# Around the end of attention: weight splits ahead of the adaLN chunks, low parts on VectorE, and 0.47 side steps per attention step for the last chunks

## The chip, the cores and the metric

One core of a Trainium2 chip runs the whole program. The metric is device time in microseconds of one execution; three runs of the kernel before gave 868.11 at the median (866.49 to 872.79).

## The reference, cut to what matters

The reference is one step of a two-layer trunk over 640 tokens (512 latent tokens, 128 context tokens) of width 1024. Layer 0 is gated attention with 16 query heads over 4 key/value heads, layer 1 a gated linear recurrence. Each layer is modulated by shift, scale and gate that come from a conditioning vector (adaLN):

```python
mod = jax.nn.silu(cond) @ w + b                 # w: 1024 x 3072, per layer
sh, sc, g = jnp.split(mod, 3, axis=-1)
h = x * (1.0 + sc) + sh
q, k, v, gate = split(h @ w_in)                  # q: 1024 wide, k and v: 256, gate: 1024
o = softmax(q @ k.T / 8) @ v                     # latent rows read 128 context + 512 latent keys
out = (o * silu(gate)) @ w_out                   # w_out: 1024 x 1024
x = layer_norm(1.414 * x + g * out) * gain + bias
```

Layer 1 does the same with a recurrence in the place of the softmax. The outputs are the tokens after both layers, the context's keys and values, and the final states of the recurrence.

## The kernel before

All matrix products with weights are made of three passes: a number is held as a high part, rounded to a short form, and a low part, which is the rest, and TensorE adds high by high, high by low and low by high. So every weight piece and every activation has to be **split**: ScalarE (ACT) casts the high part, and another engine subtracts it from the number to get the low part. `split_piece` (L219) does this for a weight piece of 128 x 1024: it takes the next raw piece out of a queue, casts it (L225), and subtracts on the engine that it is given (L226). `split_act` (L947) does the same for activations (cast L948, subtraction L949). `split_gs` (L951) splits the gated attention output `gs`, 8 slices of 128 x 640, into `hhi` and `hlo`, and gives the subtraction to GpSimd (POOL). `wo_gen` (L939) splits the 8 pieces of the output projection `attn_w_out` (two halves `nh` of the columns, four pieces each, into the tiles `wohi` and `wolo`) and lets POOL and VectorE (DVE) take turns.

**Raw pieces** come by DMA from the SP queue in one fixed order, the list `order` (L368 to L385); `pump` issues the next load whenever fewer than five loaded pieces are waiting, into a ring of six buffers. Who takes a piece must take them in that order.

**Attention** (`att_gen`, L850) goes through four groups of heads, c = 0 to 3, which the text calls quarters; a quarter has one unit for the context tokens and eight for the latent tokens. A unit has fronts (scores `sc` on TensorE (PE) at L732 and L733, row maxima `nm` on DVE at L826, exponentials `p` on ACT at L829, reciprocals `rc` on DVE at L833, and the scaling of `p` on POOL at L834) and backs (transposes `pt` on PE at L841, which ACT or DVE copies to `pts` at L737, then products with the values, `pot` at L759, and the multiplication with the gate on DVE at L764, which finishes a part of `gs`). Fronts run two units ahead of backs.

**Side work** is woven into attention's steps: `weave(att, side, SIDE_B)` (L984) makes 0.85 steps of side work for each step of attention. The side work is a list of items in order: for c = 1, 2 and 3 the projection of the next quarter's queries (`q_gen`, products `qmm`, statistics `sq`, `ss`, `rs_t`, `rstd`, then rotation, split `qs`, transposes `qps` on PE at L589 and their copy to `X` at L591), mixed with some adaLN chunks; then item "a", the last seven adaLN chunks (`ada_gen`: products `adaps` at L266, their copy to `row` at L280, two small products at L289, results `shsc` and `gcol`), which may not start before quarter 3's backs do; then item "w" (`prefetch_gen`), which splits the first two pieces of `attn_w_out`; then item "s", the first six slices of `split_gs`.

Everything up to the block's end (L993) lies in one block whose instructions a scheduler reorders with a timeline of its own, so what the code weaves is a wish, and the order on each engine is the scheduler's. Each engine then works through its own list strictly in order.

After the block's end come the last two slices of `split_gs`, the six other pieces of `attn_w_out`, and the output projection of layer 0 (`outp`, L1005 to L1009): 24 products of 128 x 512 for each token tile `tt` and half `nh`, in the order (0,0), (1,0), (0,1), (1,1), (2,0) and so on. `Norm.part` (L1026) reads a finished half out of PSUM on DVE: `y` at L1030 multiplies it by the gate, L1031 adds the residual `x`, L1033 takes statistics. Both halves of a token tile lie in one PSUM tile. The first two pieces of `rec_w_in` (tiles `rhi` and `rlo`, the weights of layer 1) are split in the same place.

Of the kernel before, what the change touches and what calls it, by code (L numbers as in the profile page):

```python
# [40 lines left out]
D_SCALE = 2  # L41
D_OUTS = 2
SIDE_T = 1.0
SIDE_B = 0.85
MIX = 0.36
D_GLA = 6.0
D_LEV = 2.3
# [38 lines left out]
def weave(main, side, ratio):  # L86
    acc = 0.0
    for _ in main:
        acc += ratio
        while acc >= 1.0:  # L90
            acc -= 1.0
            side.step()
# [40 lines left out]
def hybrid_step(ctx: ExitStack, tc: tile.TileContext, a: dict, o: dict):  # L133
    nc = tc.nc
# [85 lines left out]
    def split_piece(hi, lo, src, lo_eng=None, pinned=False):  # L220
        pump()
        got, raw = ahead.popleft()
        assert got == src, (got, src)
        pin = tc.keep_in_program_order if pinned else lambda ins: ins
        pin(nc.scalar.copy(hi, raw))  # L225
        pin((lo_eng or nc.gpsimd).tensor_tensor(lo, raw, hi.bitcast(F32), ALU.subtract))  # L226
        pump()
# [139 lines left out]
    def ada_pieces(part):  # L367
        return [p for l, c in part for p in pieces(f"ada_w{l}", c)]  # L368
# [4 lines left out]
    for c in range(3):  # L373
        order.extend(pieces("attn_w_in", c + 1))
        order.extend(ada_pieces(ADA_B[c]))
    order.extend(ada_pieces(ADA_B[3]))
    order.extend(("attn_w_out", nh, i) for nh, i in PIECES)
    order.extend(("rec_w_in", h, i) for h in range(RH) for i in range(5))
    order.extend(("rec_w_out", nh, i) for nh, i in OUT1)
    for n, back in ((0, 2), (1, 1)):  # L380
# [196 lines left out]
    def q_split(r, tt0, n, odd, X, alloc):  # L577
        s2 = prep.tile([P, 1024], F32R, tag="s2", name="qs2", bufs=2)
        rv = view(r, 0, [[HD, 4 * n], [1, HD]])
        hv = view(s2, HD * odd, [[P, 4 * n], [1, HD]])  # L580
        nc.scalar.copy(hv, rv)
        nc.vector.tensor_tensor(view(s2, HD * (1 - odd), [[P, 4 * n], [1, HD]]), rv, hv.bitcast(F32), ALU.subtract)

        def back(i):
            pt = alloc("qps")
            pr = pt[:].bitcast(F32R)
            for h in range(4):
                s = i * 512 + h * P
                nc.tensor.transpose(pr[:, h * P:(h + 1) * P], s2[:, s:s + P], identr)  # L589
            c0 = (tt0 + i) * P  # L590
            nc.scalar.copy(X[:, :, c0:c0 + P], pt[:].rearrange("p (a b) -> p a b", a=4))  # L591
        return back
# [7 lines left out]
    def q_gen(c, X):  # L600
        w = Weights("attn_w_in", c, (nc.vector, nc.vector))
        yield
        yield
        pend = None
        for tt0, n in UNITS:
            ps = yield from tok_unit(w, tt0, n, "qmm")
            rstd = rms_stat(ps, n)
            yield
            if pend:
                for i in range(pend[1]):  # L610
                    pend[0](i)
                    yield
            else:
                yield
            yield
            qn = rms_apply(ps, n, rstd)
            r = rope_apply(qn, tt0, n, cosq, sinq, qg)
            yield
            pend = (q_split(r, tt0, n, c % 2, X, bank1), n)
        yield  # L620
        for i in range(pend[1]):
            pend[0](i)
            yield
# [315 lines left out]
    def wo_gen(layer, pieces, wpool):  # L939
        for nh, i in pieces:  # L940
            hi = wpool.tile([P, 1024], F32R, tag=f"wohi{nh}{i}", name="wohi")
            lo = wpool.tile([P, 1024], F32R, tag=f"wolo{nh}{i}", name="wolo")
            wo[nh, i] = tuple(t[:].rearrange("p (k n) -> p k n", k=2) for t in (hi, lo))
            split_piece(hi, lo, ("attn_w_out" if layer == 0 else "rec_w_out", nh, i), (nc.gpsimd, nc.vector)[i % 2])
            yield

    def split_act(dst_hi, dst_lo, src, eng=None):  # L947
        nc.scalar.copy(dst_hi, src)  # L948
        (eng or nc.vector).tensor_tensor(dst_lo, src, dst_hi.bitcast(F32), ALU.subtract)  # L949

    def split_gs(ks):  # L951
        for k in ks:
            split_act(hhi[:, k, :], hlo[:, k, :], gs[:, k, :], nc.gpsimd)
            yield

    ws = ExitStack()
# [23 lines left out]

    for c in range(1, 4):
        side.items.append((f"q{c}", mixed(q_next(c), ada_gen(ADA_B[c - 1])), lambda c=c: front_of[0] >= c - 1))
    side.items.append(("a", ada_gen(ADA_B[3]), lambda: back_of[0] == 3))
    side.items += [("w", prefetch_gen()), ("s", split_gs(range(6)), lambda: back_of[0] == 3)]  # L984
    weave(att, side, SIDE_B)
    side.finish()
    ph.close()
    right.close()
# [226 lines left out]
    for tt, nh in ((0, 0), (1, 0), (0, 1), (1, 1), (2, 0), (2, 1), (3, 0), (3, 1), (4, 0), (4, 1)):  # L1215
        if nh == 0:
            norms[tt] = Norm(0, tt)
        out_mms(norms[tt].ps[nh], tt, nh, hhi, hlo)
        norms[tt].part(nh, norms[tt].ps[nh])
        if nh == 1:  # L1220
            with tc.high_priority() if tt == TS else nullcontext():
                norms[tt].finish()
            if tt > 1:
                h1_tile(tt - 1, norms[tt - 1].y)
            elif tt == 1:
                h1_tile(0, norms[0].y)
# [375 lines left out]
```

## Time and profile before

| what | us |
|---|---|
| median of three runs | 868.11 |
| the profiled execution | 868.67 |
| its span in the profile | 866.9 |
| PE busy | 827.0 (95%) |
| DVE busy | 528.8 (61%) |
| ACT busy | 382.5 (44%) |
| POOL busy | 205.9 (24%) |
| last quarter of attention, from the first of its adaLN chunks to the output projection | 311.4 to 356.3 |

Between 500 and 800 us the share of PE's busy time is 100% in each stretch of 100 us, so what is gained or lost before comes out at the end, as long as PE has its work there. The stretch that the change touches lies between 240 and 390 us. There PE's busy share falls below 90% only in a few slices of 10 us; a table of such slices gives, for each engine, the busy time and in brackets the number of instructions, and then the TensorE clock that was granted, as a share of the full one. A list of waits tells for whom an engine stood still, in us: the total, how often, and the longest. A timeline row has the start, the busy time, the engine, the line, the operation with output and input tiles, and in square brackets the idle time just before and who ended it.

### The profile page before, as it was taken

The numbers are of one execution on the slowest core, as the hardware profiler recorded it, in microseconds if no ns is written. First come the engines' busy times: TensorE is split into PE (matmuls) and PEld (weight loads), VectorE is DVE, ScalarE is ACT, GpSimd is POOL, SyncE is SP. The second block draws the span as 40 slices with busy tenths as digits, with TensorE's granted clock in tenths as the row PEclk, the third lists the DMA queues.
The fourth block names the chain that finished last, engine by engine and source line by source line (L and its number), as shares of the span: only waits on it lengthen the run. The fifth ranks groups of instructions, "written<-read, shape, count | busy, mean of one in ns | idle before, by whom it ended". The sixth has DMA issues, their size and how long they took to land.

```text
span 866.9 us, 19259 instructions
## 1 busy us (share of the span) xinstructions
PE 827.0 (95%) x8124; PEld 739.7 (85%) x8124; DVE 528.8 (61%) x942; ACT 382.5 (44%) x756; POOL 205.9 (24%) x247
## 2 busy tenths in 40 slices
PE   5989999999999898989999999999999999999996
PEld 3669999778778766667899999999999999998886
DVE  3447535665846664567635666675848495867558
ACT  2222536554745754503244444444443454544332
POOL 0113001413414743600000040323324040502011
PEclk9999999999999999999999999999999999999999
DMA  9922112212212046251221232232224232322023
GB/s 358 411 88 86 55 68 74 99 50 99 98 49 99 1 161 229 88 228 74 83 73 50 82 96 83 79 105 70 85 68 123 62 99 81 98 74 93 8 97 122
DMA packets 29606, 89.86 MB, mean 104 GB/s; under 512 B 4336, under 2 KB 8944, under 8 KB 28496
## 3 DMA queue, kind: packets, MB, share of 16 engines
q1 hardware_dynamic: 19728, 73.08, 23.8%
q0 software_dynamic: 3168, 9.31, 3.9%
q10 hardware_dynamic: 6624, 6.24, 2.3%
q8 instruction: 64, 1.05, 0.5%
q14 instruction: 22, 0.18, 0.1%
HBM read 79.44 MB, written 9.18 MB: 102 GB/s over the span
## 4 chain that ended last, share of the span: by engine, by line
PE 83%; DVE 5%; ACT 4%; issue 4%; DMA 3%; POOL 1%; SPq 0%; ACTq 0%; DVEq 0%; POOLq 0%
PE rps L1147 7%; PE rps L1149 7%; PE rps L1148 6%; PE vgps L1137 5%; PE vgps L1139 4%; PE vgps L1138 4%; PE pot L759 4%; PE pt L841 4%; PE outp L1005 3%; PE outp L1009 2%; PE outp L1008 2%; PE adaps L266 2%; PE gps L337 2%; PE lv L1285 2%; PE gps L338 2%
## 5 line engine op out<-in xcount | busy, mean ns | idle before, releaser
L1147 PE MATMUL rps<-h1hi,rhi 128*128 128x320 f32 x368 | 118.3, 321 | 0.0
L1148 PE MATMUL rps<-h1lo,rhi 128*128 128x320 f32 x368 | 113.5, 308 | 0.0
L1149 PE MATMUL rps<-h1hi,rlo 128*128 128x320 f32 x368 | 113.4, 308 | 0.0
L226 DVE TENSOR_TENSOR rlo<-raw,rhi 128x1024 fp32r<-128x1024 f32 x32 | 44.1, 1380 | 46.0 <-ACT rhi L225 46.0
L834 POOL TENSOR_SCALAR p<-p,rc 128x640 f32<-128x640 f32 x64 | 53.2, 836 | 78.5 <-DVE rc L833 68.9
L1147 PEld LDWEIGHTS rps<-h1hi,rhi 128*128 128x128 f32 x368 | 69.2, 188 | 1.3
L1148 PEld LDWEIGHTS rps<-h1lo,rhi 128*128 128x128 f32 x368 | 69.3, 188 | 0.0
L1149 PEld LDWEIGHTS rps<-h1hi,rlo 128*128 128x128 f32 x368 | 69.1, 188 | 0.1
L829 ACT ACTIVATE p<-sc,nm 128x640 f32<-128x640 f32 x64 | 51.1, 799 | 35.4 <-DVE nm L826 29.1
L826 DVE TENSOR_REDUCE nm<-sc 128x1 f32<-128x640 f32 x64 | 51.6, 817 | 18.6 <-PE sc L733 17.9
L225 ACT CAST rhi<-raw 128x1024 fp32r<-128x1024 f32 x32 | 33.6, 1050 | 61.0 <-PE rps L1148 57.1
L1258 ACT COPY kc<-A 128x640 f32<-128x640 f32 x40 | 32.4, 811 | 52.0 <-PE lv L1285 29.7
L841 PE MATMUL pt<-ident,p 128*128 128x128 f32 x320 | 50.6, 283 | 3.2 <-ACT pts L737 1.5
L1137 PE MATMUL vgps<-rhi,h1hi 128*128 128x256 f32 x180 | 51.2, 284 | 0.0
L1138 PE MATMUL vgps<-rlo,h1hi 128*128 128x256 f32 x180 | 50.5, 280 | 0.0
L1139 PE MATMUL vgps<-rhi,h1lo 128*128 128x256 f32 x180 | 50.2, 279 | 0.0
L737 ACT COPY pts<-pt 128x512 f32<-128x512 f32 x64 | 36.6, 588 | 27.8 <-PE pt L841 27.5
L841 PEld LDWEIGHTS pt<-ident,p 128*128 128x128 f32 x320 | 37.7, 146 | 12.5 <-issue 8.9
L194 POOL TENSOR_TENSOR rstdo<-rs_t,mhalf 128x5 f32<-128x5 f32 x8 | 9.5, 1192 | 162.3 <-DVE rs_t L193 162.3
L732 PE MATMUL sc<-kk,X 128*128 128x320 f32 x128 | 42.8, 344 | 2.9 <-ACT p L829 2.8
L1137 PE MATMUL vgps<-wspare,h1hi 128*128 128x256 f32 x140 | 41.5, 297 | 0.0
L337 PE MATMUL gps<-hhi,whi 128*128 128x320 f32 x128 | 40.1, 313 | 0.7 <-ACT X L591 0.4
(273 smaller groups left out, 2413.2 us busy)
## 6 DMA issues: line engine op xcount, KB each, us to landing
raw<-in_rec_w_in SPq DMA_DIRECT2D x40, 512.0 KB, 4.0
raw<-in_ada_w SPq DMA_DIRECT2D x32, 512.0 KB, 3.9
raw<-in_ada_w SPq DMA_DIRECT2D x8, 1024.0 KB, 10.8
raw<-in_attn_w_in SPq DMA_DIRECT2D x16, 512.0 KB, 4.7
raw<-in_attn_w_out SPq DMA_DIRECT2D x8, 512.0 KB, 5.9
raw<-in_rec_w_out SPq DMA_DIRECT2D x8, 512.0 KB, 3.7
h<-in_xT SPq DMA_DIRECT2D x8, 320.0 KB, 9.2
x1d<-y SPq DMA_DIRECT2D x5, 512.0 KB, 2.6
```

Source lines behind the costliest of these rows:

```text
L226: pin((lo_eng or nc.gpsimd).tensor_tensor(lo, raw, hi.bitcast(F32), ALU.subtract))
L337: nc.tensor.matmul(ps[:, :320], w.hi(k)[:, c], hhi[:, k, t], start=(k == 0), stop=False)
L826: nc.vector.tensor_reduce(nm[:, 0:1], sc[:, :, :320], AX.XY, ALU.max, negate=True)
L829: nc.scalar.activation(halves(p[:]), sc[:, :, :320], AF.Exp, bias=nm[:, 0:1], accum_out=su[:, 0:1])
L834: nc.gpsimd.tensor_scalar(p, p, rs[:, 0:1], 1.0, ALU.mult, ALU.mult)
L841: nc.tensor.transpose(pt[:, i * 256 + q * P:i * 256 + (q + 1) * P], ps[q][:, (k0 + i) * P:(k0 + i + 1) * P], ident)
L1137: nc.tensor.matmul(out, h1hi[:, k, t], hi, start=(k == 0), stop=False)
L1138: nc.tensor.matmul(out, h1hi[:, k, t], lo, start=False, stop=False)
L1139: nc.tensor.matmul(out, h1lo[:, k, t], hi, start=False, stop=(k == KT - 1))
L1147: nc.tensor.matmul(ps[:, j, :320], hi[:, k, :], h1hi[:, k, t], start=(k == 0), stop=False)
L1148: nc.tensor.matmul(ps[:, j, :320], hi[:, k, :], h1lo[:, k, t], start=False, stop=False)
L1149: nc.tensor.matmul(ps[:, j, :320], lo[:, k, :], h1hi[:, k, t], start=False, stop=(k == KT - 1))
```

## The change

The change has five parts.

1. The list of loads has the first two pieces of `attn_w_out` ahead of the last seven adaLN chunks (14 pieces) instead of behind them, and item "w", which splits them, comes ahead of item "a" and without a condition. It can so run as soon as quarter 3's queries are done.
2. All low parts of `attn_w_out` and of `gs` are subtracted on DVE: `wo_gen` passes `nc.vector`, `split_gs` no engine, for which `split_act` takes DVE.
3. Items "a" and "s" become one, `last_gen`, which makes one slice of `split_gs` after every second step of the adaLN chunks.
4. While that item is the only one left, the side work makes 0.47 steps for each step of attention, before that 0.85 as now. `q_gen` makes two more empty steps ahead of its last transposes.
5. The first two token tiles' `Norm.part` gets high priority after the block.

```diff
-SIDE_B = 0.85
+SIDE_B = (0.85, 0.47)
...
 def weave(main, side, ratio):
     acc = 0.0
     for _ in main:
-        acc += ratio
+        acc += ratio() if callable(ratio) else ratio
...
+    order.extend(("attn_w_out",) + p for p in PIECES[:2])
     order.extend(ada_pieces(ADA_B[3]))
-    order.extend(("attn_w_out", nh, i) for nh, i in PIECES)
+    order.extend(("attn_w_out",) + p for p in PIECES[2:])
...
             pend = (q_split(r, tt0, n, c % 2, X, bank1), n)
+        yield
+        yield
         yield
...
-            split_piece(hi, lo, ("attn_w_out" if layer == 0 else "rec_w_out", nh, i), (nc.gpsimd, nc.vector)[i % 2])
+            split_piece(hi, lo, ("attn_w_out" if layer == 0 else "rec_w_out", nh, i), nc.vector)
...
-            split_act(hhi[:, k, :], hlo[:, k, :], gs[:, k, :], nc.gpsimd)
+            split_act(hhi[:, k, :], hlo[:, k, :], gs[:, k, :])
...
-    side.items.append(("a", ada_gen(ADA_B[3]), lambda: back_of[0] == 3))
-    side.items += [("w", prefetch_gen()), ("s", split_gs(range(6)), lambda: back_of[0] == 3)]
-    weave(att, side, SIDE_B)
+    side.items.append(("w", prefetch_gen()))
+    def last_gen(ada):
+        splits = split_gs(range(6))
+        for n, _ in enumerate(ada):
+            yield
+            if n % 2:
+                next(splits, None)
+        yield from splits
+
+    side.items.append(("a", last_gen(ada_gen(ADA_B[3])), lambda: back_of[0] == 3))
+    weave(att, side, lambda: SIDE_B[len(side.items) < 2])
...
-        norms[tt].part(nh, norms[tt].ps[nh])
+        with tc.high_priority() if tt < 2 else nullcontext():
+            norms[tt].part(nh, norms[tt].ps[nh])
```

What the scheduler makes of it is seen at three places. The first is POOL from the second last statistics of quarter 3's queries on, around the slices of `hlo`; before, this stood there:

```order
L194 TENSOR_TENSOR rstd<-rs_t,mhalf 128x8
L834 TENSOR_SCALAR p<-p,rc 128x640 x4
L949 TENSOR_TENSOR hlo<-gs,hhi 128x640
L834 TENSOR_SCALAR p<-p,rc 128x640
L949 TENSOR_TENSOR hlo<-gs,hhi 128x640 x3
L834 TENSOR_SCALAR p<-p,rc 128x640 x2
L194 TENSOR_TENSOR rstd<-rs_t,mhalf 128x4
L834 TENSOR_SCALAR p<-p,rc 128x640 x2
L949 TENSOR_TENSOR hlo<-gs,hhi 128x640
```

All slices of `hlo` have left POOL, and the same seven scalings stand between the two statistics. POOL has this now (line numbers of the changed kernel are 3 higher here):

```order
L194 TENSOR_TENSOR rstd<-rs_t,mhalf 128x8
L837 TENSOR_SCALAR p<-p,rc 128x640 x7
L194 TENSOR_TENSOR rstd<-rs_t,mhalf 128x4
L837 TENSOR_SCALAR p<-p,rc 128x640 x3
L798 TENSOR_TENSOR pp<-pp,rcp 128x512
L837 TENSOR_SCALAR p<-p,rc 128x640 x16
```

From there to the block's end POOL does nothing but scale. The second place is ACT, where the first two casts `wohi` stand. Before, they are in the last quarter, among the last exponentials:

```order
L829 ACTIVATE p,su<-sc,nm 128x640 x4
L225 CAST wohi<-raw 128x1024
L737 COPY pts<-pt 128x512 x2
L225 CAST wohi<-raw 128x1024
L829 ACTIVATE p,su<-sc,nm 128x640 x2
L737 COPY pts<-pt 128x512 x2
```

Now they stand some 15 rows earlier on ACT, right behind the last copy `X` of quarter 3's queries and ahead of the context unit's exponentials `pp`:

```order
L740 COPY pts<-pt 128x512
L592 CAST X_2731<-qps 128x4x128
L225 CAST wohi<-raw 128x1024 x2
L740 COPY pts<-pt 128x512 x2
L792 ACTIVATE pp,sup<-pscp,nmp 128x128 x4
L740 COPY pts<-pt 128x512
```

Both casts have moved from the middle of the last quarter to its start, ahead of two copies `pts`. The third place is DVE from the last gate multiplication of attention, over the block's end, to the first read of the output projection. Before:

```order
L764 TENSOR_TENSOR gs<-pot,gs 128x256
L993 UNCONDITIONAL_BRANCH
L226 TENSOR_TENSOR wolo<-raw,wohi 128x1024 x3
L226 TENSOR_TENSOR rlo<-raw,rhi 128x1024
L1074 TENSOR_TENSOR modA<-shsc_85,lnc 128x16
L1075 TENSOR_TENSOR modB<-shsc_85,lnc 128x16
L226 TENSOR_TENSOR rlo<-raw,rhi 128x1024
L1076 TENSOR_TENSOR modB<-modB,shsc_85 128x16
L1030 TENSOR_TENSOR y<-outp,gate_108 128x512
```

Three of the six low parts `wolo` stood here and three on POOL, and the read `y` came behind both `rlo`. Now DVE has:

```order
L767 TENSOR_TENSOR gs<-pot,gs 128x256
L1004 UNCONDITIONAL_BRANCH
L952 TENSOR_TENSOR hlo<-gs,hhi 128x640
L226 TENSOR_TENSOR wolo<-raw,wohi 128x1024
L952 TENSOR_TENSOR hlo<-gs,hhi 128x640
L226 TENSOR_TENSOR wolo<-raw,wohi 128x1024 x5
L1041 TENSOR_TENSOR y<-outp,gate_108 128x512
L1085 TENSOR_TENSOR modA<-shsc_85,lnc 128x16
L1086 TENSOR_TENSOR modB<-shsc_85,lnc 128x16
L226 TENSOR_TENSOR rlo<-raw,rhi 128x1024
```

Six `wolo` and two `hlo` stand ahead of `y`, and both `rlo` have gone behind it.

## The prediction

> **What bounds the kernel now.** I read the page first, then the list of PE's waits from 240 to 420 us, then a table of 10 us stretches, and last the timeline around the longest waits. The page's head and one stretch far behind the change:
>
> ```profile
> span 866.9 us, 19259 instructions
> ```
>
> ```profile
> 500.00:600.00 100.00, 100.00 (x1289) 96.95 (x1288) 62.37 (x100) 43.73 (x95) 25.03 (x38) 1.00 0.29 83
> ```
>
> PE is busy for all of those 100 us at the full clock. So TensorE bounds the program, and time saved ahead of 400 us stays saved, since nothing behind it waits for a clock time. What PE waited for in the stretch that the change touches (total, times, longest):
>
> ```profile
> PE outp L1005 <- DVE y L1030: 4.2, 2, 3.8
> PE qps L589 <- DVE qs L582: 2.7, 1, 2.7
> PE adaps L289 <- DVE gcol L300: 2.6, 1, 2.6
> PE sc L732 <- ACT p L829: 0.9, 4, 0.3
> PE pt L841 <- ACT pts L737: 0.7, 2, 0.5
> PE outp L1005 <- DVE gs L764: 0.5, 1, 0.5
> PE pot L759 <- DVE pts L737: 0.5, 1, 0.5
> ```
>
> Three single waits, 3.8, 2.7 and 2.6 us, are most of it; everything else is half a microsecond at a time. The waits cost more than themselves where the clock falls behind them (the last three numbers of a row are clock, DMA share, GB/s):
>
> ```profile
> 290.00:300.00 10.00, 7.06 (x59) 5.65 (x59) 6.55 (x16) 6.82 (x17) 8.85 (x9) 1.00 0.01 2
> 330.00:340.00 10.00, 7.38 (x67) 5.82 (x67) 5.48 (x12) 5.18 (x9) 3.96 (x3) 0.92 0.77 246
> 340.00:350.00 10.00, 9.52 (x71) 7.14 (x70) 3.50 (x9) 5.68 (x13) 2.39 (x3) 0.91 0.22 82
> 370.00:380.00 10.00, 8.14 (x28) 6.51 (x29) 5.77 (x9) 0.00 (x0) 0.00 (x0) 0.83 0.71 274
> ```
>
> The clock's loss from 330 to 350 is (0.08 + 0.09) x 10 = 1.7 us, and from 370 to 380 it is 0.17 x 10 = 1.7 us. Behind the 2.7 us wait, between 290 and 300, it stays at 1.00.
>
> **The change part by part.** I go by the three waits, last first, because the last is the surest.
>
> *D, the output projection.* The timeline there, and the durations that the same instructions have elsewhere (shortest, median, longest in ns):
>
> ```profile
> 355.78 0.42 DVE L764 TENSOR_TENSOR gs<-pot,gs 128x256 f32<-128x256 f32 x1 [2.48 <-PE pot L759]
> 358.61 7.79 DVE L226 TENSOR_TENSOR wolo<-raw,wohi 128x1024 fp32r<-128x1024 f32 x3 [2.41 <-ACT wohi L225]
> 366.33 3.39 DVE L226 TENSOR_TENSOR rlo<-raw,rhi 128x1024 fp32r<-128x1024 f32 x1
> ...
> 371.03 0.68 DVE L1030 TENSOR_TENSOR y<-outp,gate 128x512 f32<-128x512 f32 x1
> ```
>
> ```profile
> 361.92 6.71 POOL L226 TENSOR_TENSOR wolo<-raw,wohi 128x1024 fp32r<-128x1024 f32 x2
> ```
>
> ```profile
> 356.25 0.50 PE L1005 MATMUL outp<-wohi,hhi 128*128 128x512 f32 x1 [0.53 <-DVE gs L764]
> ...
> 371.86 0.47 PE L1005 MATMUL outp<-wohi,hhi 128*128 128x512 f32 x1 [3.77 <-DVE y L1030]
> ```
>
> ```profile
> L226 DVE TENSOR_TENSOR rlo<-raw,rhi x32: 1209/1222/3392, 366.3 to 776.4; 128x1024 fp32r<-128x1024 f32 x32
> ...
> L226 DVE TENSOR_TENSOR wolo<-raw,wohi x4: 1597/2248/3436, 333.6 to 363.0; 128x1024 fp32r<-128x1024 f32 x4
> ```
>
> ```profile
> L460 DVE TENSOR_TENSOR hlo<-h,hhi x8: 815/826/1362, 11.5 to 58.0; 128x640 fp32r<-128x640 f32 x8
> ```
>
> PE does halves (0,0) and (1,0) from 356.25 to 371.86 - 3.77 = 368.09, then stands still until `y` of (0,0) is read, although its product was done about 5.9 us earlier: `y` is behind three `wolo` and two `rlo`, at 2.6 and 3.4 us each while POOL subtracts beside them, against a median of 1.22. After the change DVE begins at 355.78 + 0.42 = 356.20 with 2 x 0.83 + 6 x 1.22 = 9.0 us of low parts (POOL is empty), so they end at 365.2 and `y` at 365.9, 2.2 us ahead of 368.09. Nothing in (0,0) waits: the first `wolo` is there at 356.2 + 0.83 + 1.22 = 358.3 and wanted after 12 of 24 products, at 356.25 + 2.95 = 359.2; the second, behind another `hlo`, at 360.3 and wanted after 18, at 360.7. That is the thinnest margin; if it is missed by some tenths, that much is lost. Next late is `y` of (1,0), wanted when (0,1) ends at about 374; ahead of it stand two `rlo`, whose pieces load no later than now, because their buffers come free by the first `wolo`. The priority costs nothing, since only `y` of (0,0) moves and the `rlo` behind it are wanted only when all of `outp` is done. So the 3.8 us go, and with them the dip behind: D = 3.8 + 1.7 = 5.5. Bounds: 3.8 (the dip stays) and 5.5.
>
> *B, the two early pieces of `attn_w_out`.*
>
> ```profile
> 330.64 1.05 ACT L225 CAST wohi<-raw 128x1024 fp32r<-128x1024 f32 x1 [2.13 <-DMA raw<-in_attn_w_out]
> ```
>
> ```profile
> 333.63 1.60 DVE L226 TENSOR_TENSOR wolo<-raw,wohi 128x1024 fp32r<-128x1024 f32 x1 [2.16 <-ACT wohi L225]
> ```
>
> ```profile
> 336.82 0.61 PE L289 MATMUL adaps<-small,row 128*128 128x2 f32 x4 [2.62 <-DVE gcol L300]
> ```
>
> The casts wait for a load, DVE's subtraction waits for the cast, two row maxima and a `gcol` stand behind it, and PE waits for that. With the casts gone from there, the wait and, I take it, the dip go: B = 2.6 + 1.7 = 4.3; bounds 0 (another wait in its place) and 4.3. The two loads now stand ahead of 14 adaLN loads on SP; the DMA share of 0.01 between 290 and 300 shows room, and the adaLN loads, wanted at about half the pace, have more time than now.
>
> The Trainium skill (TensorE: Matmul & The Clock Gate, What's actually happening) has the clock halve after an idle window of about 3.4 us. By that rule the 2.62 us would not be the dip's cause, the dip might stay, and the sum would be 1.7 us smaller; the rows are on both sides, a dip after 2.62 and none after 2.72, and I keep the row at the place.
>
> *C, the spread chunks.* Seven chunks that fill PE from 311 to 338 now reach to the last units, where PE waited 0.5 + 0.5 us for copies `pts`. PE's work is the same. The last wait (`pot` for `pts`) has no filler either way. C = 0.5; bounds 0 and 1.
>
> *A, POOL and ACT at the start of the last quarter.*
>
> ```profile
> 287.11 5.02 POOL L949 TENSOR_TENSOR hlo<-gs,hhi 128x640 fp32r<-128x640 f32 x3
> ...
> 293.65 1.01 POOL L194 TENSOR_TENSOR rstd<-rs_t,mhalf 128x4 f32<-128x4 f32 x1
> ```
>
> ```profile
> 286.32 0.16 DVE L297 TENSOR_TENSOR shsc<-adaps,small 128x4 f32<-128x4 f32 x1 [1.08 <-PE adaps L289]
> 287.52 0.82 DVE L826 TENSOR_REDUCE nm<-sc 128x1 f32<-128x640 f32 x1 [1.04 <-PE sc L733]
> ```
>
> ```profile
> 298.33 0.52 PE L589 MATMUL qps<-identr,qs 128*128 128x128 f32 x4 [2.72 <-DVE qs L582]
> ...
> 301.80 2.38 PE L759 MATMUL pot<-pts,vv 128*64 128x256 f32 x20
> ```
>
> ```profile
> 298.88 0.59 ACT L591 CAST X<-qps 128x512 fp32r<-128x512 f32 x1 [1.53 <-PE qps L589]
> 299.39 1.07 ACT L737 COPY pts<-pt 128x512 f32<-128x512 f32 x2
> ```
>
> Three `hlo` hold up POOL's scalings and `rstd`, and over `qs` the transposes at 298.33. Without them `rstd` can come some 1.5 us earlier, and the steps behind it on DVE no longer run beside POOL's subtractions. But DVE takes four `hlo` here, 4 x 0.83 = 3.3 us against 1.08 + 1.04 = 2.1 us of idle time, so row maxima come up to 1.2 us later. I take 2.0 of the 2.7 us as gone. Then the new casts: two of 1.05 us on ACT ahead of the copies `pts`, so `pts` end where they end now, at 300.5, or 0.1 later, while PE would be ready for `pot` at 301.8 - 2.0 = 299.8; it waits 0.8. A = 2.0 - 0.8 = 1.2. Bounds: a gain of 2.7 (all of the wait, casts hidden) and a loss of 1.2 (the late maxima alone).
>
> The Trainium skill (SBUF — State Buffer, Who interferes with whom) has a DVE operation with two SBUF inputs and a GpSimd operation that reads SBUF block each other. This speaks against the change where POOL still scales: each `hlo` could hold up a scaling, and A would come near its bad bound, 2.4 us off the sum; for D, where POOL is empty, it speaks for it, as the 2.6 against 1.22 us do.
>
> Two more empty steps in `q_gen` and some reordered transposes around 245 us I cost at nothing: PE has projection products beside them and no wait over 0.3 us there.
>
> **Sum.** 1.2 + 4.3 + 0.5 + 5.5 = 11.5 us. The profiled execution took 868.67, 1.8 above its span and 0.56 above the median of 868.11: 868.67 - 11.5 = 857.2, and against the median 856.6. I say 857.
>
> **The rivals.** *The last quarter stays bound by its chain of dependent steps* (0.2): with fewer chunks per step PE waits for exponentials and scalings where it now has chunks, and B and C (4.8) come back as small waits; 868.7 - 1.2 - 5.5 = 862. For it: the 0.9 us of waits for `p` without filler. Against it: these are 0.3 at most each.
>
> *The dips stay* (0.12), because short waits at other phases bring them: 857.2 + 3.4 = 860.6. For it: the clock's dips don't follow from the waits' lengths alone.
>
> *Slower: the low parts cost on DVE what they cost now* (0.05), because it is the place and not POOL that makes them slow. At 7.79 / 3 = 2.6 and 1.36 (the longest `hlo`), DVE ends at 356.2 + 6 x 2.6 + 2 x 1.36 = 374.5 and `y` at 375.2, 3.5 after 371.71 now, and the dip stays; the six low parts at the start of the quarter cost 2 x 1.4 + 4 x 0.53 = 4.9 more, and A's gain goes; B and C still give 4.8: 868.7 + 3.5 + 4.9 - 4.8 = 872.3. It decides from 6w + 2h = 11 on, that is w = 1.56 with h = 0.83. Against it: 32 `rlo` with a median of 1.22, the slow ones beside POOL's.
>
> That the change does nothing of the kind (0.02) is excluded by the order on DVE; other small mixtures hold the remaining 0.03.
>
> **Chances and range.** The forecast has 0.58; its own range, by A between 2.7 and -1.2 and C up to 1, is 854.5 to 859.5. The range to 863 takes in the second and third case, and 854 is the best of A and C against the median; what is left out is about 0.1 to 0.15. Faster by over 1% (about what can be told from no change) means under 859.4: nearly all of the forecast and a few hundredths of the others, 0.6. Slower by over 1%, over 876.8, would take the slow rival and something more, 0.03. The rest, 0.37, lies within 1%.
>
> **What would show it.** D: no PE wait for `y` over 0.5 us, `wolo` on DVE at 1.2, the clock at 1.00 where `outp` runs. B: no wait of PE for `gcol`, no cast that waits for a load in the last quarter, clock 1.00 there. A: `qps` waiting under 1 us, and a new wait of `pot` or `pt` for `pts` under 1 us. C: no more than 0.5 us of waits behind the last chunk. Wrong would be it if PE's busy share from 305 to 350 falls below 95% without one long wait (the first rival), or if `wolo` takes over 1.56 us.

## The result and the profile after

The changed kernel takes 856.37 us (median of five runs, 855.59 to 859.21) against 868.86 us for the kernel before (five runs, 866.49 to 872.79). The ratio is 0.9857, with a 95% interval of 0.9823 to 0.9891: faster by 1.4%. The forecast was 857, with a range of 854 to 863. The profiled execution took 855.59 us, against 857.2 by the sum.

The span fell from 866.9 to 853.6 us. PE's waits between 230 and 410 us (total, times, longest, in us), which answer to the list in the prediction:

```profile
PE sc L735 <- ACT p L832: 0.9, 4, 0.3
PE outp L1016 <- DVE y L1041: 0.7, 2, 0.4
PE outp L1016 <- DVE gs L767: 0.5, 1, 0.5
PE pot L762 <- DVE pts L740: 0.5, 1, 0.5
PE pt L844 <- ACT pts L740: 0.5, 2, 0.3
PE pt L844 <- ACT X L592: 0.4, 1, 0.4
PE qps L590 <- DVE rc L836: 0.3, 1, 0.3
PE qps L590 <- DVE pts L740: 0.2, 1, 0.2
```

The three long waits (3.8, 2.7 and 2.6 us) are gone and nothing over half a microsecond has come in their place. The table of 10 us stretches (busy time and instructions of PE, PE's weight loads, DVE, ACT and POOL, then clock, DMA share, GB/s) shows the dips gone too:

```profile
290.00:300.00 10.00, 9.48 (x76) 7.48 (x78) 7.28 (x18) 8.86 (x18) 4.43 (x6) 1.00 0.01 2
...
330.00:340.00 10.00, 10.00 (x96) 7.12 (x95) 5.94 (x17) 5.46 (x12) 3.45 (x5) 1.00 0.63 214
340.00:350.00 10.00, 8.89 (x72) 6.14 (x71) 3.06 (x8) 4.58 (x8) 0.54 (x1) 1.00 0.25 92
...
360.00:370.00 10.00, 9.66 (x42) 7.48 (x41) 5.42 (x9) 0.00 (x0) 0.00 (x0) 1.00 0.78 309
```

The clock is 1.00 in each of them; before it was 0.92 and 0.91 between 330 and 350 and 0.83 between 370 and 380.

To see where the time went I cut each trace at the start of five products that every kernel here has in the same order: the first context scores `pscp` of quarter 2 (A starts there) and of quarter 3 (B and C), the first `outp` (D), and in layer 1 the first `vgps` and the first `rps`. The times between them, from the timelines of PE, in us:

| | before | after | less by | forecast |
|---|---|---|---|---|
| start to `pscp` of quarter 2 | 243.70 | 243.60 | 0.10 | 0 |
| to `pscp` of quarter 3 | 56.01 | 54.32 | 1.69 | A 1.2 |
| to the first `outp` | 56.54 | 51.22 | 5.32 | B + C 4.8 |
| to the first `vgps` | 66.44 | 61.16 | 5.28 | D 5.5 |
| to the first `rps` | 15.89 | 15.02 | 0.87 | none |
| to the end | 428.32 | 428.28 | 0.04 | 0 |

Together that is 13.3 us of span; the medians differ by 12.5. The last stretch, 428 us in which PE is the bound, is the same in both, so what was gained ahead did stay gained. The fifth line was not in the forecast.

### The profile page after: what moved, and what is told of

It is laid out like the page before. It is cut to its first block, busy times and chain, and to the rows that moved or that the text cites. A ratio compares the mean times of both kernels' runs of the same rounds, so it can differ in the third digit from the quotient of the medians.

```text
span 853.6 us, 19263 instructions
## 1 busy us (share of the span) xinstructions
PE 822.8 (96%) x8124; PEld 737.2 (86%) x8124; DVE 528.7 (62%) x954; ACT 382.3 (45%) x756; POOL 182.8 (21%) x235
## 4 chain that ended last, share of the span: by engine, by line
PE 84%; DMA 6%; DVE 4%; ACT 3%; issue 1%; POOL 0%; SPq 0%; DVEq 0%; ACTq 0%
PE rps L1158 7%; PE rps L1160 7%; PE rps L1159 7%; PE vgps L1148 5%; PE vgps L1150 4%; PE vgps L1149 4%; PE pot L762 4%; PE pt L844 4%; PE outp L1016 4%; PE outp L1019 3%; PE outp L1020 3%; PE gps L337 2%; PE lv L1297 2%; PE gps L338 2%; PE gps L339 2%; DMA h<-in_xT 2%
## 5 line engine op out<-in xcount | busy, mean ns | idle before, releaser
L837 POOL TENSOR_SCALAR p<-p,rc 128x640 f32<-128x640 f32 x64 | 55.2, 866 | 84.3 <-DVE rc L836 73.0
L226 DVE TENSOR_TENSOR rlo<-raw,rhi 128x1024 fp32r<-128x1024 f32 x32 | 41.9, 1311 | 46.0 <-ACT rhi L225 46.0
```

Of the source, the lines that this page charges most:

```text
L837: nc.gpsimd.tensor_scalar(p, p, rs[:, 0:1], 1.0, ALU.mult, ALU.mult)
```

## The experiments

The theory on trial is that of the prediction: three separate waits with three separate causes, two of them with a dip of the clock behind, and each taken away by one part of the change. Its rivals are that one part does all of it, that parts only help together, and that the gain has another cause than the one named (POOL's own time, the slower chunks, a load). So I undid parts, did parts alone, and made one wait again at chosen lengths. In the tables the stretches are named as the terms: A up to `pscp` of quarter 3, BC up to `outp`, D up to `vgps`, E up to `rps`. A and BC repeat from trace to trace to within some hundredths of a microsecond where nothing is changed in them (last section), so they decide where medians can't. D repeats less well: 61.16 and 61.40 in two traces of the changed kernel, 60.73 to 61.67 over all kernels whose long wait for `y` is gone. Differences of less than half a microsecond are not read from it.

**The priority alone.** Added to the kernel before:

```diff
-        norms[tt].part(nh, norms[tt].ps[nh])
+        with tc.high_priority() if tt < 2 else nullcontext():
+            norms[tt].part(nh, norms[tt].ps[nh])
```

> The kernel before with the high priority for the first two token tiles' part alone; POOL keeps its low parts. On DVE the read y of (0,0) moves from behind both rlo to right behind the three wolo. Three stretches tell the cases apart: from the context scores of quarter 3 (299.7 us before, 297.9 after) to the first outp (356.3, 349.1), and from there to the first product of layer 1 (422.7, 410.3): 56.5 and 66.4 us before, 51.2 and 61.2 after. My theory, that the place of y in DVE's list makes the wait: the wolo end at 366.4 as before, y at 367.1, 1 us ahead of 368.1; the wait of 3.8 us and the dip go, the last stretch is 61.2 us, and the whole is 5.3 us faster than before. Rival, that the low parts have to leave POOL: the last stretch stays at 66 us and the time within 1 us of before.

Measured: 865.11 us, ratio 0.9957 (0.9937 to 0.9977); stretches A 56.02, BC 56.15, D 60.89, E 16.35. PE's waits in this kernel:

```profile
PE qps L589 <- DVE qs L582: 2.7, 1, 2.7
PE adaps L289 <- DVE gcol L300: 2.5, 1, 2.5
...
PE outp L1005 <- DVE y L1030: 0.4, 1, 0.4
```

All of D is there (60.89 against 66.44), and A is as before. BC is 0.39 us shorter than before, although the wait for `gcol` (2.5) and the dip behind it are still there; why, this run doesn't show. Three `wolo` at the slow rate ahead of `y` are harmless once the two `rlo` stand behind it. So the wait came from the order on DVE, not only from the slow subtractions.

**The change without the priority.** The same lines the other way round, taken out of the changed kernel.

> The changed kernel without the high priority; on DVE y of (0,0) stands behind six wolo and both rlo again. My theory, that either half of the change at this place is enough: the casts rhi end at 358.1 in the changed kernel, so the second rlo ends near 359.4 and y near 360.3, 0.7 us ahead of 361.0, where PE asks for it; the last stretch stays at 61.2 us and the time within 1 us of the changed kernel. Rival, that the priority carries the gain: PE waits 3 us or more for y, the clock dips, and the time is 4 to 5.5 us above the changed kernel.

Measured: 857.03 us, ratio 0.9858 (0.9828 to 0.9889); A 54.31, BC 51.23, D 61.04, E 15.02. D is as good without the priority. With all low parts on DVE the `rlo` cost 1.22 us each, and PE waits only 0.28 us for `y` of (0,0), which the expectation had 0.7 early. The faster subtractions are the smaller part of that: from the end of the last `gs` to the start of `y` DVE took 14.83 us before and 10.86 here, and 2.41 of these 3.97 us are the time that it stood idle for a cast `wohi` (the row at 358.61 in the prediction), in which it now makes a slice and the first `wolo`. Two parts of the change each take away the whole of D, and the second of them then adds nothing: what such parts bring alone can't be added.

**The slices of `gs` back on POOL.** In the changed kernel:

```diff
-    def split_gs(ks):
+    def split_gs(ks, eng=None):
...
-            split_act(hhi[:, k, :], hlo[:, k, :], gs[:, k, :])
+            split_act(hhi[:, k, :], hlo[:, k, :], gs[:, k, :], eng)
...
-        splits = split_gs(range(6))
+        splits = split_gs(range(6), nc.gpsimd)
```

> The changed kernel with the first six slices of split_gs subtracted on POOL as before. My theory, that POOL's list held up rstd and with it the last query transposes: the wait of qps for qs comes back with 2 to 3 us, the context scores of quarter 3 start at 299.7 instead of 297.9, and the time is 1.8 us above the changed kernel; the later stretches stay at 51.2 and 61.2 us. Rival, that DVE pays for the slices what POOL paid: the context scores start before 298.3 and the time is within 0.5 us of the changed kernel.

Measured: 860.78 us, ratio 0.99 (0.9872 to 0.9929); A 56.01, BC 51.23, D 61.54, E 16.25. A is 56.01, as before the change, so its gain is gone; BC, in which one of the six slices lies, holds at 51.23. That A agrees to the hundredth is in part luck: PE's wait for `qs` comes back with 1.8 us and not with the 2.7 of before (2 to 3 expected), and PE is busy for 52.99 us in A instead of 52.43. POOL's timeline shows how; its rows read like those of the kernel before:

```profile
288.79 5.03 POOL L952 TENSOR_TENSOR hlo<-gs,hhi 128x640 fp32r<-128x640 f32 x3
...
295.31 1.03 POOL L194 TENSOR_TENSOR rstd<-rs_t,mhalf 128x4 f32<-128x4 f32 x1
```

The changed kernel has this on POOL:

```profile
285.57 2.68 POOL L837 TENSOR_SCALAR p<-p,rc 128x640 f32<-128x640 f32 x1 [1.12 <-DVE rc L836]
...
290.68 0.80 POOL L837 TENSOR_SCALAR p<-p,rc 128x640 f32<-128x640 f32 x1 [0.65 <-DVE rs_t L193]
291.45 1.01 POOL L194 TENSOR_TENSOR rstd<-rs_t,mhalf 128x4 f32<-128x4 f32 x1
```

`rstd` comes at 291.45 instead of 293.65 before, and the transposes `qps` at 295.74 instead of 298.33. One scaling did pay, 2.68 us instead of 0.80, beside these on DVE:

```profile
285.32 0.80 DVE L952 TENSOR_TENSOR hlo<-gs,hhi 128x640 fp32r<-128x640 f32 x1
286.05 0.15 DVE L297 TENSOR_TENSOR shsc<-adaps,small 128x4 f32<-128x4 f32 x1
286.12 1.54 DVE L952 TENSOR_TENSOR hlo<-gs,hhi 128x640 fp32r<-128x640 f32 x2
```

The scaling ends at 288.25, 0.6 us after DVE is through with the slices (287.66), and the slices keep their 0.8 us each. The Trainium skill (SBUF — State Buffer, Who interferes with whom) has a DVE operation with two SBUF inputs contend with a GpSimd operation that reads SBUF, for a pair of ports that only one of them can hold; the rows agree with it. POOL itself waited 1.0 us for the next `rc` after it, and PE has no wait over 0.3 us at this place.

**The early pieces alone.** The kernel before, with its engines and its pace, but with the two pieces early:

```diff
+    order.extend(("attn_w_out",) + p for p in PIECES[:2])
     order.extend(ada_pieces(ADA_B[3]))
-    order.extend(("attn_w_out", nh, i) for nh, i in PIECES)
+    order.extend(("attn_w_out",) + p for p in PIECES[2:])
...
-    side.items.append(("a", ada_gen(ADA_B[3]), lambda: back_of[0] == 3))
-    side.items += [("w", prefetch_gen()), ("s", split_gs(range(6)), lambda: back_of[0] == 3)]
+    side.items += [("w", prefetch_gen()), ("a", ada_gen(ADA_B[3]), lambda: back_of[0] == 3)]
+    side.items.append(("s", split_gs(range(6)), lambda: back_of[0] == 3))
```

> The kernel before with the two early pieces of attn_w_out loaded and split ahead of the last seven adaLN chunks, at the old pace of 0.85 and with the low parts on the engines of before. My theory, that the late load made the wait of 2.6 us and the dip behind it: PE's wait for gcol goes, the clock is 1.00 throughout the quarter, the middle stretch falls from 56.5 to about 52.2 us, the last stays at 66.4, and the time is 4.3 us below before. Rival, that the chunks have to be spread too: with all chunks done early PE waits for exponentials and copies in the quarter's last units, the middle stretch stays above 55 us and the time is within 2 us of before.

Measured: 865.14 us, ratio 0.994 (0.9921 to 0.9959); A 56.02, BC 52.07, D 66.43, E 15.01. Its waits, and its stretches around the old place of the casts and in the output projection:

```profile
PE outp L1006 <- DVE y L1031: 4.2, 2, 3.8
PE qps L590 <- DVE qs L583: 2.7, 1, 2.7
```

```profile
330.00:340.00 10.00, 10.00 (x92) 8.25 (x92) 6.15 (x17) 5.26 (x12) 3.18 (x4) 1.00 0.60 210
...
360.00:370.00 10.00, 6.20 (x21) 4.63 (x20) 8.00 (x11) 0.00 (x0) 1.57 (x1) 0.83 0.98 374
```

The wait for `gcol` and its dip are gone, worth 56.54 - 52.07 = 4.47 us; the other two waits stand untouched. The two casts, which ACT now makes from 296.77 to 298.77, cost next to nothing there: A is 56.02, and of the quarter's first 10.08 us after `pscp` PE is busy for 9.87.

**One pace for all the side work.** In the changed kernel:

```diff
-SIDE_B = (0.85, 0.47)
+SIDE_B = (0.85, 0.85)
```

> The changed kernel with the pace of 0.85 kept for the last seven chunks. The stretch from the context scores of quarter 3 to the first outp took 56.5 us before, 52.1 with the two early pieces alone, and 51.2 in the changed kernel. My theory, that the pace itself is worth the rest, some waits of half a microsecond behind the last chunk: 52.0 us here, and the time 0.8 us above the changed kernel. Rival, that the pace is worth nothing and the low parts on DVE brought the rest: 51.2 us and the time of the changed kernel. Second rival, that the chunks at the old pace now meet the splits between them on DVE: over 53 us.

Measured: 856.30 us, ratio 0.9842 (0.9797 to 0.9887); A 54.33, BC 50.59, D 61.47, E 16.25. BC is 0.63 us better at the old pace, so spreading the chunks costs time instead of bringing 0.5. The waits in this stretch don't tell why. The changed kernel has 0.5 for `outp`, 0.5 for `pot` (both in its list above) and one of 0.3 for `p`. With one pace it is:

```profile
PE outp L1016 <- DVE gs L767: 0.5, 1, 0.5
PE pot L762 <- DVE pts L740: 0.5, 1, 0.5
PE pt L844 <- ACT pts L740: 0.2, 1, 0.2
```

The wait of `pot` for `pts` and that of the first `outp`, at the quarter's end, are there in both. PE's busy time in the stretch is 49.72 us in the changed kernel, 49.26 with one pace and 50.65 with the early pieces alone, and what is left is idle: 1.50, 1.33 and 1.42. Most of the difference between the three lies in how long PE is busy with the same work, not in its waits; by what in the order, these runs don't show. E of 16.25 is another matter, below.

**The empty steps taken out of `q_gen`.** In the changed kernel, without the two more `yield`.

> The changed kernel without the two more empty steps in q_gen. I had costed them at nothing: the stretch from the context scores of quarter 2 to those of quarter 3 (56.0 us before, 54.3 after) stays at 54.3 within 0.3, the next one at 51.2, the time within 0.5 us of the changed kernel. Rival, that the empty steps let the last query transposes wait behind useful work and so brought the 1.7 us: 56 us, with a wait of qps for qs of 2 us or more.

Measured: 856.06 us, ratio 0.9832 (0.9777 to 0.9888); A 53.54, BC 51.63, D 61.67, E 16.11. A is better by 0.78 without them, BC worse by 0.41. "Costed at nothing" holds to 0.4 us in sum, but the empty steps do move time over the border.

**A wait of chosen length for `y`.** The kernel without the priority, in which DVE repeats the subtraction of the last piece, so that `y` comes later; the repeats write the same values, so nothing is left out. First with two more:

```diff
+        if src == ("attn_w_out", 1, 3):
+            for w in [1024, 1024]:
+                nc.vector.tensor_tensor(lo[:, :w], raw[:, :w], hi[:, :w].bitcast(F32), ALU.subtract)
```

> The changed kernel without the priority, and with the subtraction of the last piece of attn_w_out made twice more, so that DVE reads y of (0,0) later and PE waits for it for about 2.4 us, in the place where it waited 3.8 before. It asks what brings the clock down: after 2.6 us of waiting for gcol it fell to 0.91 for 20 us of the table, after 2.7 us of waiting for qs it stayed at 1.00. Theory a, that the work around the wait decides and not its length alone, thin products before and behind gcol, full ones here: the clock stays at 1.00 with 2.4 us, and the stretch from outp to layer 1 is 61.1 + 2.4 = 63.5 us. Theory b, that any wait from 2.4 us on can bring it down, by where it falls: clock 0.83 to 0.9 in one row, and about 65 us.

and then with `[1024, 1024, 512]`:

> As the run with a wait of about 2.4 us, with half a subtraction more, so that PE waits about 3.1 us. Theory a: the bound lies between 2.7 and 3.8 us among full products, and this run shows on which side 3.1 is: 64.2 us with the clock at 1.00, or 65.9 with a dip. Theory b: a dip, 65.9 us.

Measured, one run each, 860.1 and 859.67 us; A 54.34 and 54.32, BC 51.22 and 51.22, D 63.18 and 65.30, E 15.01 in both. With the shorter delay PE waits 2.56 us and the clock stays at 1.00:

```profile
365.56 0.48 PE L1019 MATMUL outp<-wohi,hhi 128*128 128x512 f32 x1 [2.56 <-DVE y L1044]
```

```profile
360.43:363.84 3.41, 2.57 (x12) 1.72 (x10) 3.41 (x5) 0.80 (x1) 0.00 (x0) 1.00 0.93 336
363.84:367.25 3.41, 1.69 (x7) 1.42 (x8) 2.75 (x4) 0.00 (x0) 0.00 (x0) 1.00 1.00 387
```

With the longer delay it waits 3.15 us, and the clock falls to one half:

```profile
363.60 0.48 PE L1019 MATMUL outp<-wohi,hhi 128*128 128x512 f32 x1 [3.15 <-DVE y L1044]
...
364.84 0.41 PE L1023 MATMUL outp<-wohi,hlo 128*128 128x512 f32 x1
365.07 0.60 PE L1019 MATMUL outp<-wohi,hhi 128*128 128x512 f32 x1
365.48 0.63 PE L1022 MATMUL outp<-wolo,hhi 128*128 128x512 f32 x1
```

```profile
361.68:365.09 3.41, 1.49 (x7) 1.25 (x8) 3.06 (x5) 0.00 (x0) 0.00 (x0) 1.00 1.03 406
365.09:368.50 3.41, 3.41 (x10) 2.64 (x9) 1.65 (x3) 0.00 (x0) 0.00 (x0) 0.50 0.71 282
```

It doesn't fall at once: the products go on 0.23 us apart for 1.5 us, and then 0.43 apart, for 3.41 us. In D the last 0.6 us of waiting cost 65.30 - 63.18 = 2.1 us.

It would be rash to read a bound between 2.56 and 3.15 us from these two runs, because the wait's place counts as well as its length. Cut finely, each of the 29 dips that the fourteen traces have before 840 us is one stretch of 3.41 us at a clock of 0.50, and where a trace has several, they begin whole multiples of 3.41 us apart: before the change at 38.00, 338.38 and 372.51 (88 and 10 times 3.41), without the priority at 36.72, 46.96 and 186.91 (3 and 41 times). So in these traces the clock goes by a grid of 3.41 us that runs through, wherever a wait begins; the rows above are cut on it. A dip fills the grid's stretch behind one in which PE stood still for much of the time. With the shorter delay the wait is divided between two stretches, with 2.57 and 1.69 us of busy PE, and none follows; with the longer one 1.49 us is left in one, and a dip follows. Before the change 1.56 us stood ahead of the dip behind `gcol` and 0.65 ahead of the one behind `y`, while the wait of 2.72 us for `qs` was divided and left 1.61.

Waits of equal length can go either way, as a place between 182 and 187 us shows. PE has the same three waits there, of 0.70, 0.52 and 0.38 us, in the changed kernel and in the one without the priority. In the first the clock stays at 1.00, and a border of the grid, counted on from its dip at 37.32, falls between them at 184.09. In the second all three lie in one stretch, and the clock falls behind it. The first of the waits in either kernel, and the two stretches of the second:

```profile
182.81 0.63 PE L844 MATMUL pt<-ident,p 128*128 128x128 f32 x4 [0.70 <-DVE gate L310]
```

```profile
184.37 0.63 PE L844 MATMUL pt<-ident,p 128*128 128x128 f32 x4 [0.70 <-DVE gate L310]
```

```profile
183.50:186.91 3.41, 1.81 (x15) 1.38 (x15) 3.17 (x8) 2.43 (x5) 0.96 (x2) 1.00 0.52 159
186.91:190.32 3.41, 3.41 (x16) 2.58 (x18) 2.06 (x5) 0.77 (x2) 0.85 (x1) 0.50 0.47 150
```

How little work brings a dip is not settled: 1.81 us of busy PE did here, and 1.61 did not ahead of `qs`, so busy time alone isn't the measure, and no run here moved a wait of fixed length along the grid. The Trainium skill (TensorE: Matmul & The Clock Gate, What's actually happening) has the clock halve after an idle window of about 3.4 us that runs on its own. The halving (0.43 against 0.23 us), the length and the free run agree; but PE was not idle through any of the stretches named here, it worked for 0.65 to 1.81 us in those ahead of a dip.

**The masks without a cast.** E differs between runs in a stretch that the change doesn't touch. On DVE the cast of a constant, the masks of layer 1, stands ahead of the last token tile's statistics. The timelines before and after:

```profile
426.14 0.24 DVE L1246 CAST masks<-mst 128x160 uint8<-128x160 f32 x1 [1.10 <-DMA mst<-in_masks]
```

```profile
412.72 0.24 DVE L1258 CAST masks<-mst 128x160 uint8<-128x160 f32 x1
```

With the slices on POOL it waited again, for 1.61 us. Where the load lands late, all of DVE stands behind it, and PE then waits 0.6 to 1.1 us for `y` of the norm. To test it, the changed kernel gets the masks as bytes straight from memory:

```diff
-    mst = g1.tile([P, 5, 32], F32, tag="kt", name="mst")
-    nc.scalar.dma_start(mst, a["masks"])
-    nc.vector.tensor_copy(masks, mst)
+    nc.scalar.dma_start(masks, a["masks"])
...
-    masks = np.stack(masks, axis=1).astype(np.float32)
+    masks = np.stack(masks, axis=1).astype(np.uint8)
```

> The changed kernel with the masks of the recurrence stored as bytes, so that they are loaded in their final form and DVE makes no cast of them. In four of the six traces so far that have it, DVE waits 1.1 to 1.6 us for that load, ahead of the last token tile's statistics, and PE waits 0.6 to 1.1 us for that tile's y; in the others the load lands in time. My theory: the stretch from layer 1's first product to its first rps is 15.0 us in every run, as it was in the changed kernel's trace, so this profile shows no gain, and the median falls by 0 to 0.9 us, by how often the load was late. Rival, that another load takes its place: 15.9 us or more.

Beside it ran the changed kernel once more:

> The changed kernel once more, beside the one with the masks as bytes, and as a second trace of the same program. The stretches should be 54.3, 51.2 and 61.2 us again; the one from layer 1's first product to its first rps is 15.0 or 15.9 to 16.4 us, by whether the masks' load lands in time.

Measured: with bytes 857.43 us, ratio 0.9858 (0.9841 to 0.9876), and the changed kernel 858.00, ratio 0.9869 (0.9851 to 0.9887). E is 15.01 with bytes and 15.00 in this trace of the changed kernel, in which the load happened to land in time. The medians don't separate the two. Eleven traces are of kernels with the cast. In six of them DVE had no such wait, and E is 15.00 to 15.02; in the five others (before, the priority alone, slices on POOL, one pace, no empty steps) it waited 1.1 to 1.7, and E is 15.89 to 16.35. The load took 1.8 to 2.2 us from its issue to its landing in the six and 3.2 to 3.8 in the five. E thus goes with the wait for this load; why the load is late in some traces, no run shows.

**The parts put together.** The changed kernel with one pace and the masks as bytes, and the same without the empty steps as well:

> The changed kernel with the pace of 0.85 for all chunks and the masks stored as bytes. From the traces: 54.3 us from quarter 2's context scores to quarter 3's, 50.6 to the first outp (51.2 with the pace of 0.47), 61.1 to layer 1's first product, 15.0 to the first rps: 0.6 us less than the changed kernel's 181.7 for the four stretches in its first trace, 181.0. If the pace's 0.6 us hang on what the masks' load did in that run, the second stretch is 51.2 again. In the medians against before 0.6 us will not be told from none.

> As the run with the pace of 0.85 and the masks as bytes, without the two more empty steps in the query projections. Alone their removal took the first stretch from 54.3 to 53.5 us and the second from 51.2 to 51.6. If both effects add, the stretches are 53.5, 51.0, 61.1 and 15.0, 180.6 in all against 181.7 in the changed kernel's first trace; if the scheduler makes another order of it, the second is over 51.6 and nothing is won.

Measured: 855.53 us, ratio 0.9847 (0.9822 to 0.9871), with A 54.30, BC 50.58, D 60.88, E 15.01; and 856.61 us, ratio 0.9854 (0.983 to 0.9879), with 53.52, 51.34, 60.99, 15.01. The first adds up to 180.77 against 181.72 and 181.93 in the two traces of the changed kernel: about 1 us better by stretches, of which the last stretch takes back 0.3 (428.63 against 428.28 and 428.33), and not distinguishable by medians. The second gives 0.76 in BC for 0.78 gained in A, so leaving out the empty steps is worth nothing. No run here clearly beats the changed kernel.

## Why the prediction was right, and where a step was off

*D, right in size and cause, with one thing overlooked.* Forecast 5.5, measured 5.28. The rows of DVE at the place, as the prediction asked for them:

```profile
349.00 0.81 DVE L952 TENSOR_TENSOR hlo<-gs,hhi 128x640 fp32r<-128x640 f32 x1
349.86 1.23 DVE L226 TENSOR_TENSOR wolo<-raw,wohi 128x1024 fp32r<-128x1024 f32 x1
351.00 0.82 DVE L952 TENSOR_TENSOR hlo<-gs,hhi 128x640 fp32r<-128x640 f32 x1
351.74 5.76 DVE L226 TENSOR_TENSOR wolo<-raw,wohi 128x1024 fp32r<-128x1024 f32 x5
357.42 0.68 DVE L1041 TENSOR_TENSOR y<-outp,gate 128x512 f32<-128x512 f32 x1
```

And the durations of all `wolo` (shortest, median, longest in ns):

```profile
L226 DVE TENSOR_TENSOR wolo<-raw,wohi x8: 1214/1219/1228, 298.4 to 356.3; 128x1024 fp32r<-128x1024 f32 x8
```

They take 1.21 to 1.23 us, which ends the rival that the place and not POOL makes them slow (it needed 1.56). `y` ends at 358.10. With the 11.84 us that (0,0) and (1,0) took before, PE wants it at 349.14 + 11.84 = 360.98: 2.9 us of slack, forecast 2.2. The thin margin of the second `wolo` held. Overlooked was that the two parts of the change at this place are alternatives, as the first two experiments show. The forecast took `y` to be late through five operations on DVE and called all five slow; the second `rlo` took 1.21 us (it starts at 369.81, when POOL is done), so it was four. Moving the two `rlo` behind `y`, or taking the low parts off POOL, is enough.

*B, right.* Forecast 4.3, measured alone 4.47. I took the row at the place, a dip after 2.62 us, and the dip did go with the wait: the clock is 1.00 there in every kernel that has the early pieces, and 0.91 and 0.92 in the priority alone, which hasn't. Whether a wait of 2.6 us has a dip behind it in every execution, two traces that have it don't say, as its place on the grid counts.

*C, wrong in sign.* The forecast gave 0.5, because spread chunks would cover one wait of `pt` for `pts` in the last units; the last wait, `pot` for `pts`, it left standing, and that stayed at 0.5. Two steps failed. The wait to be covered was mostly gone without the spreading: it was 0.48 before, and with the early pieces alone, at the old pace, it is 0.17:

```profile
347.70 0.63 PE L841 MATMUL pt<-ident,p 128*128 128x128 f32 x4 [0.48 <-ACT pts L737]
```

```profile
340.93 1.07 PE L842 MATMUL pt<-ident,p 128*128 128x128 f32 x8 [0.17 <-ACT pts L738]
```

And "PE's work is the same" did not mean the same time: PE is busy for 0.46 us longer at the slower pace (49.72 against 49.26), and the pace alone costs 0.63. The bounds (0 to 1) were too narrow below. BC nonetheless came out 0.5 above the forecast. With 4.47 from the early pieces and -0.63 from the pace, 5.32 - 4.47 + 0.63 = 1.48 is left for the rest of the change (low parts on DVE, slices mixed with chunks, empty steps), if these parts add up. Of this the slices' engine is nothing (51.23 with POOL) and the empty steps are 0.4 at the new pace; the remaining 1.1 were not separated. That BC came out near its forecast is in part luck.

*A, right in cause, under-sized.* Forecast 2.0 - 0.8 = 1.2, measured 1.69. The first term was about right: `rstd` came 2.2 us earlier, the wait ahead of the last `qps` fell from 2.72 to 0.16, and PE's idle time in the whole stretch from 3.58 to 1.42, that is by 2.16. The other two terms were wrong and partly made up for each other. The empty steps, costed at nothing, cost: PE was busy for 0.47 us longer than before (52.90 against 52.43), and without the empty steps A is 53.54, a gain of 2.47 (BC loses 0.41 of that). And the 0.8 for the casts ahead of `pts` was not there. The wait that is left, and ACT's casts:

```profile
295.74 0.54 PE L590 MATMUL qps<-identr,qs 128*128 128x128 f32 x4 [0.16 <-DVE pts L740]
...
297.92 0.31 PE L735 MATMUL pscp<-kk,X 128*128 128x128 f32 x1
```

```profile
297.26 2.03 ACT L225 CAST wohi<-raw 128x1024 fp32r<-128x1024 f32 x2
299.15 1.10 ACT L740 COPY pts<-pt 128x512 f32<-128x512 f32 x2
```

The copies `pts` do come behind both casts, but PE, which starts on the context unit's scores at 297.92, is busy for 9.97 of the 10.08 us from there to 308: its products `pot`, one group of 20 before, now come as 12 at 299.58 and 8 at 301.61, with a `pt` between them, and don't wait. The slowing beside DVE's slices that spoke against this part was seen (2.68 us), but on one scaling that nothing waited for.

*The rivals.* The last quarter did not stay bound by its chain: from 305 to 350 PE is busy for 43.5 of 45 us (97%; under 95% would have spoken for it), and 9.73 to 10.00 of each 10 us from 310 to 340, the least in this one:

```profile
320.00:330.00 10.00, 9.73 (x92) 7.00 (x93) 5.72 (x14) 4.80 (x11) 2.98 (x4) 1.00 0.62 203
```

The dips did not stay, by the clock in the first section; what stood for that rival, that dips don't follow from the waits' lengths alone, is borne out by the dips at 186 us.

*Not in the sum.* E, 0.87 us, goes with a load's landing, early or late in kernels with the change and without it, so I count it as no effect of the change. It accounts for half of the 1.8 us by which the span fell more than forecast (13.3 against 11.5); A and BC have 0.5 each, and D gave back 0.2.

## What to carry to other kernels

Where an engine works strictly in order, look at what stands ahead of the one instruction that the bound engine waits for: moving it past two subtractions brought the same 5.3 us or so as taking the low parts off POOL, which let DVE start at once and make each of them in 1.22 us, and doing both brought no more. A dip cost about 1.7 us here, half of 3.41, on top of the wait ahead of it; bringing a wait of 3.15 us down to 2.56 saved 2.1 in one pair of runs, but whether a dip follows a wait hangs on its place on the grid too. Filler work that is spread more evenly helps only if PE's waits lie where it is put; here one was nearly gone by another part of the change, and the others lay at the end, where there was no filler either way.

## What the runs showed of the hardware that was not expected

The start varies by itself by more than most parts of the change. Up to `pscp` of quarter 2 the traces took between 241.10 us (the early pieces alone) and 246.54 (without the priority), by parts of the programs that the experiments leave alone. It goes with the number of dips. The two traces with no dip there took 241.10 and 241.56 us, the six with one, at 37 to 38 us, 243.46 to 244.24, and the six with three, at 36, 46 and 186 us or just behind, 245.66 to 246.54. In the early pieces alone the clock is 1.00 from 20 to 240 us. Without the priority:

```profile
20.00:40.00 20.00, 17.77 (x98) 13.59 (x99) 10.75 (x19) 4.91 (x6) 3.63 (x4) 0.92 1.03 410
40.00:60.00 20.00, 16.75 (x110) 11.76 (x110) 9.77 (x18) 5.21 (x6) 3.45 (x3) 0.91 0.45 169
```

From 20 to 60 us that is (0.08 + 0.09) x 20 = 3.4 us of clock, and another 0.09 x 20 = 1.8 from 180 to 200 us, 5.2 of the 5.4 in all. The waits themselves don't differ so: PE's longest from 20 to 62 us, for the cast `hhi`, is 1.85 us in the twelve traces with dips, and 2.15 and 2.17 in the two without one. So where the waits fell on the grid of 3.41 us fits these rows and their lengths don't; no run here set the place on purpose. The medians' spread goes the same way: the five executions of the changed kernel took 855.59, 855.63, 856.37, 858.07 and 859.21 us at mean clocks of 0.996, 0.996, 0.994, 0.992 and 0.991. By contrast the stretches behind the start repeat: A is 54.30 to 54.34 in the eight traces that have the low parts on DVE and the empty steps, and BC is 51.21 to 51.23 in the six of them that also have the slower pace. That is why an effect of 0.6 us could be read from single traces while medians of four or five runs, whose times spread over 2 to 6 us, could not show it.
